# A two-layer hybrid decoder on one core: the 16 operand tiles of the activations, each 64 bytes further into its 512 bytes than the last

## The chip, the cores and the metric

One core of a Trainium2 chip runs the whole program. The metric is device time in microseconds, from one launch to its end. In the profile PE is TensorE, PEld its weight loads, DVE VectorE, ACT ScalarE, POOL GpSimd and SP SyncE, which issues the loads of the weights.

## What is computed

Two decoder layers on 512 tokens of 1024 channels, float32. Each layer adds half of a SwiGLU feed-forward net (FFN) of the normalized residual, then a mixer (a state-space scan, sliding-window attention and a spatial gating unit, side by side), then half of a second FFN; a last RMSNorm ends it. From the reference:

```python
def swiglu(x, w_gate, w_up, w_down):
    return (jax.nn.silu(x @ w_gate) * (x @ w_up)) @ w_down
...
    for l in range(DEPTH):
        x = x + 0.5 * swiglu(rmsnorm(x, ffn1_norm[l]), ffn1_w_gate[l], ffn1_w_up[l], ffn1_w_down[l])
        h = rmsnorm(x, mix_norm[l])
        proj = h @ w_in[l]
...
        x = x + jnp.concatenate([y_ssd, y_att, y_sgu], axis=-1) @ w_out[l]
        x = x + 0.5 * swiglu(rmsnorm(x, ffn2_norm[l]), ffn2_w_gate[l], ffn2_w_up[l], ffn2_w_down[l])
    return rmsnorm(x, final_norm)
```

The width of a FFN is 2816 = 22 x 128.

## The kernel before

The residual stays in SBUF as eight tiles xT (L66), 128 channels on the partitions by 512 tokens. Weights come as tiles of 128 output channels: `load` (L106) fetches 128 x 1024 float32 into one of five buffers raw, and `split` (L119) makes of it a pair whi (ScalarE, L128) and wlo (VectorE, L129), four buffers each, whose sum is the weight. Activations are split the same way: `split_x` (L135) takes two buffers from `xtile` (L132) and writes xhi (ScalarE, L137) and xlo (VectorE, L138). Both kinds are float32r. `product` (L142) then sums, for each chunk of 128 input channels, three matmuls into one PSUM bank: xhi with whi (L148), xlo with whi (L149), xhi with wlo (L151). In each, the weights are the stationary operand (128 x 128, 512 bytes on a partition, loaded by a weight load of its own) and the activations the moving one (512 columns, 2048 bytes on a partition).

A stage takes 16 tiles from `xtile`, a hi and a lo for each of eight chunks, always in the order hi 0, lo 0, hi 1, lo 1 and so on: `prepare` (L196) and `prepare_first` (L204) for the two FFNs and the mixer's input projection, `finish` (L524) for its output projection. `in_products` (L212) takes the weight tiles one after another through the eight chunks: 44 tiles in a FFN, 20 (and one of 16 columns, wdt, L657) in a mixer's input projection, eight in its output projection. The FFN's second product uses the same `product` with tiles h (L310), 4096 bytes with hi and lo side by side, as the moving operand: 22 chunks for each of eight output tiles. In the last FFN that is replaced by `down_final` (L702): h is the stationary operand there, in pieces of 128 tokens, and whi or wlo the moving one (L722 to L724); it also takes two tiles fw from the activations' buffers for the weights of the last norm, which VectorE reads at L734.

Layout in SBUF: pools lie one behind another in the order const, wp, xp, rp, and then ff (an FFN) or mp (a mixer). wp holds 13 tiles of 4096 bytes (raw, whi, wlo). xp holds the eight xT and the 16 activation tiles, 2048 bytes each. rp holds five tiles of 2048 bytes and two tiles rcol of 16 bytes, which take 32 each. The tiles of ff, h among them, are multiples of 2048 bytes. The order of the instructions and all waits between engines come from the framework, which follows tiles: a tile that reuses a buffer waits for the last reader of the one before.

Of the kernel before, what the change touches and what calls it, by code (L numbers as in the profile page):

```python
"""Two hybrid decoder layers (macaron SwiGLU, SSD | sliding-window attention | chunked SGU) on one core.

The residual lives in SBUF, channels on partitions. Every weight product takes both operands as an
exact pair hi + lo of float32r numbers and sums hi*hi + hi*lo + lo*hi in float32 in PSUM. The scale
of a token's RMSNorm is applied to the product's rows instead of to its operand.
"""
# [11 lines left out]
F32 = mybir.dt.float32  # L18
F32R = mybir.dt.float32r
# [3 lines left out]
PSUM = bass.MemoryType.PSUM  # L23
# [12 lines left out]

# columns of the table of per-channel vectors, 128 channels each
COLS = ("ffn1_norm", "mix_norm", "ffn2_norm", "ssd_norm", "attn_out_norm", "sgu_out_norm", "sgu_ln_w", "conv_b",
# [3 lines left out]
    [0, 16, 16, 16, 8, 4, 4, 4, 16, 64, 8]).tolist()  # L42
# the order in which the tiles of the input projection are taken
XBC_AT, GV_AT, U_AT, Z_AT = 4, 12, 14, 16
# [3 lines left out]
def trunk(ctx: ExitStack, tc: tile.TileContext, a: dict, out: bass.AP, phases=None):  # L48
# [42 lines left out]
    def attention_bias(pool, tags):  # L91
        """One row of biases by distance, skewed through DRAM into a Toeplitz band."""
        relx = rp.tile([33, 4], F32, name="relx", tag="rcol", bufs=2)
        nc.gpsimd.memset(relx, 1.0)
        nc.sync.dma_start(out=relx[0:32, :], in_=a["rel_bias"])
        ohx = pool.tile([33, 384], F32, name="ohx", tag=tags[0])
        nc.sync.dma_start(out=ohx, in_=a["onehot"])
        for h in range(4):
            b = bank()
            nc.tensor.matmul(b[:, 0:384], relx[:, h:h + 1].broadcast_to([33, P]), ohx, start=True, stop=True)  # L100
            ext = pool.tile([P, 384], F32, name="ext", tag=tags[1 + h % 2])
            nc.vector.tensor_copy(out=ext, in_=b[:, 0:384])
            nc.gpsimd.dma_start(out=skew[h].rearrange("(q i) -> q i", i=385)[:, 0:384], in_=ext)

# [1 line left out]
    def load(view):  # L106
        """Weights as they come, up to 1024 columns."""
        n = view.shape[-1]
        raw = wp.tile([P, 1024], F32, name="raw", tag="raw", bufs=RAW)[:, :n]
        nc.sync.dma_start(out=raw, in_=view)  # L110
        return raw
# [3 lines left out]
    def pinned(i):  # L115
        """At the start the engines take things in the order of the loads."""
        return order[0](i)

    def split(raw, n=P, mid=None):  # L119
        """Columns of weights as hi and lo, [P, chunks, n]; in halves if there is something to do between them."""  # L120
        m = raw.shape[1]
        hi = wp.tile([P, 1024], F32R, name="whi", tag="whi", bufs=4)[:, :m]
        lo = wp.tile([P, 1024], F32R, name="wlo", tag="wlo", bufs=4)[:, :m]
        for i in range(2 if mid else 1):
            if i:
                mid()
            c = slice(i * m // 2, (i + 1) * m // 2) if mid else slice(0, m)
            pinned(nc.scalar.copy(out=hi[:, c], in_=raw[:, c]))  # L128
            pinned(nc.vector.tensor_tensor(out=lo[:, c], in0=raw[:, c], in1=hi[:, c].bitcast(F32), op=ALU.subtract))  # L129
        return tuple(t.rearrange("p (k n) -> p k n", n=n) for t in (hi, lo))  # L130

    def xtile(nm):  # L132
        return xp.tile([P, T], F32R, name=nm, tag="xs", bufs=16)

# [7 lines left out]
    def product(ps, wt, x, ks, first, last):  # L142
        """ps += W[k].T X[k] for (i, k) in ks; wt = (hi, lo) with k's place i on axis 1, x = list of (hi, lo)."""
        whi, wlo = wt
        mm = None
        for i, k in ks:
            xh, xl = x[k]
            nc.tensor.matmul(ps, whi[:, i, :], xh, start=(k == first), stop=False)  # L148
            mm = nc.tensor.matmul(ps, whi[:, i, :], xl, start=False, stop=(wlo is None and k == last))  # L149
            if wlo is not None:  # L150
                mm = nc.tensor.matmul(ps, wlo[:, i, :], xh, start=False, stop=(k == last))  # L151
        latest[0] = mm.ins
# [3 lines left out]
    def behind():  # L156
        """What follows goes to TensorE behind the products so far."""
        return tc.issue_after(latest[0])

    class Stat:  # L160
        """Sum of squares of channel chunks as they come, then 1/sqrt(mean + eps) per token."""
        def __init__(self):
# [23 lines left out]
        def spread(self):  # L186
            """1/sqrt(...) of every token on all partitions, in PSUM."""
            r = self.r
            bc = bank()
            with behind():  # L190
                for c in range(NB):
                    nc.tensor.matmul(bc[:, c * P:(c + 1) * P], r[:, c:c + 1].broadcast_to([P, P]), ident,  # L192
                                     start=True, stop=True)
            return bc

    def prepare(wrow):  # L196
        """The current residual times the norm's weight as hi/lo operands, and its sum of squares."""
        st = Stat()
        xs = [split_x(xT[j], vcol(wrow + j)) for j in range(KD)]
        for j in range(KD):  # L200
            st.add(xT[j])
        return xs, st

    def prepare_first(wrow, js, xs, st):  # L204
        """The same for chunks js while the residual comes in."""
        for j in js:
            xs.append(split_x(xT[j], vcol(wrow + j)))
        if js[-1] == KD - 1:
            for j in range(KD):
                st.add(xT[j], nc.gpsimd if j < 4 else nc.vector)  # L210

    def in_products(tiles, xs, emit, hooks, levels=None, feed=None, ready=2, lead=3):  # L212
        """One product for each maker in tiles (-> (hi, lo), rows); the first lead ones go through the operand's
        chunks level by level, so that the last chunks may come late. hooks[v, n] is called before tile n's
        part of level v, feed before a level but the first; what emit needs is there before tile number ready ends."""
        levels = levels or [list(range(KD - 2)), [KD - 2, KD - 1]]
# [33 lines left out]

# [1 line left out]
    def ffn(l, which, first=False, fin=False):  # L252
# [82 lines left out]

# [1 line left out]
    def mixer(l):  # L337
# [3 lines left out]
        with tc.tile_pool(name="mp", bufs=1) as mp:  # L341
# [5 lines left out]

            # parameters of this layer
            bm = mp.tile([P, 4, 256], F32, name="bm")
# [24 lines left out]

# [1 line left out]
            dt, av, acs, cd, dtde = (small(n, 32) for n in ("dt", "av", "acs", "cd", "dtde"))  # L376
# [152 lines left out]

# [1 line left out]
            kT = t512("kT")  # L531
# [68 lines left out]

# [1 line left out]
            gn = mp.tile([P, NB, 256], F32, name="gn")  # L602
# [47 lines left out]

# [1 line left out]
            def mk_cols(i):  # L652
# [37 lines left out]

# [1 line left out]
            def mk_o(j):  # L692
# [9 lines left out]
    def down_final(dv, h):  # L702
        """out = rmsnorm(x + h W) with tokens on partitions, all of its sums in PSUM at once."""
        fw = [xp.tile([P, 512], F32, name=f"fw{i}", tag="xs", bufs=16) for i in range(2)]
        for i in range(2):
# [54 lines left out]
def one_hot_buckets():  # L760
    """Which bucket a distance has (the reference's static table), as one-hot columns between masked ends."""
    buckets, far = 32, 128
    n = np.arange(P)
    exact = buckets // 2
    large = exact + (np.log(np.maximum(n, 1) / exact) / np.log(far / exact) * (buckets - exact)).astype(np.int32)
    bucket = np.where(n < exact, n, np.minimum(large, buckets - 1))
    oh = np.zeros((33, 3 * P), np.float32)
    oh[32, :P] = NEG
    oh[32, 2 * P:] = NEG
    oh[bucket[::-1], P + n] = 1.0  # L770
    return oh


def laid_out(inputs):
    """The inputs as the kernel reads them: weights in tiles of 128 output channels, each with its chunks of
    128 input channels one after another on a partition; the residual with channels on partitions."""
    inp = {n: np.asarray(v) for n, v in inputs.items()}

    def tiles(w):
        """[..., K, N] -> [..., N / P, P, K / P * P]"""  # L780
        k, n = w.shape[-2:]
# [41 lines left out]
```

## Time and profile before

| | us |
|---|---|
| median of 2 runs | 1887.45 |
| range of the runs | 1886.72 to 1888.17 |
| span of the profiled execution | 1886.8 |

The profile is of one execution. Its page gives the busy time of every engine, the chain of work that ended last and the costliest groups of instructions; the trace behind it can be asked for the instructions in order of time (the timeline), for a table of stretches, and for one line of the code. Matmuls overlap at their ends, so the busy time of one is longer than the distance from its start to the start of the next.

### The profile page before, as it was taken

How to read it: one execution, taken by the hardware profiler on the slowest of the kernel's cores; microseconds unless marked ns; L12 is line 12 of the kernel's file. 1: busy time of each engine (PE TensorE's matmuls, PEld its weight loads, DVE VectorE, ACT ScalarE, POOL GpSimd, SP SyncE). 2: the span in 40 equal slices, each digit the busy share in tenths (PEclk: the TensorE clock that was granted, in tenths of full speed). 3: DMA queues.
4: the chain of work that ended last, by engine and by line, in shares of the span. 5: the costliest groups of instructions: out<-in, count | busy, mean ns of one | idle time of the engine just before them, and what ended most of it. 6: DMA issues, size and time to landing. Idle time of an engine off the chain costs nothing.

```text
span 1886.8 us, 21326 instructions
## 1 busy us (share of the span) xinstructions
PE 1868.9 (99%) x8608; PEld 1527.5 (81%) x8608; DVE 874.1 (46%) x1203; ACT 632.5 (34%) x854; POOL 127.9 (7%) x126
## 2 busy tenths in 40 slices
PE   8999999999999999999999999999999999999998
PEld 6888888877888888888888888887778888888886
DVE  6444433368855433433344344333787554444222
ACT  4323322247443322322223233223564432232112
POOL 2000000010221000000000000001102200000000
PEclk9999999999999999999999999999999999999999
DMA  5222333342222232233322323333422223223231
GB/s 210 100 100 90 98 92 93 97 141 70 79 87 99 91 101 99 89 92 99 102 91 99 101 91 93 92 90 110 123 89 69 90 90 101 96 94 101 79 100 45
DMA packets 54926, 182.78 MB, mean 97 GB/s; under 512 B 7211, under 2 KB 9196, under 8 KB 54828
## 3 DMA queue, kind: packets, MB, share of 16 engines
q1 hardware_dynamic: 49484, 172.37, 28.2%
q0 software_dynamic: 1920, 6.59, 1.2%
q10 hardware_dynamic: 3424, 2.46, 0.4%
q8 instruction: 68, 1.11, 0.2%
q14 instruction: 30, 0.25, 0.0%
HBM read 178.48 MB, written 2.92 MB: 96 GB/s over the span
## 4 chain that ended last, share of the span: by engine, by line
PE 94%; DVE 2%; DMA 1%; issue 1%; ACT 1%; POOL 0%; POOLq 0%; SPq 0%; ACTq 0%; DVEq 0%
PE accb L148 28%; PE accb L149 28%; PE accb L151 28%; PE mxb L723 1%; PE mxb L724 1%; PE mxb L722 1%; PE accb L723 1%; PE accb L722 1%; PE accb L724 1%; DMA acb<-arow 1%; PE mxb L179 1%; PE mxb L492 0%; PE mxb L192 0%; PE mxb L588 0%; PE mxb L641 0%
## 5 line engine op out<-in xcount | busy, mean ns | idle before, releaser
L148 PE MATMUL accb<-xhi,whi 128*128 128x512 f32 x1856 | 728.5, 393 | 5.9 <-ACT xhi L137 5.9
L149 PE MATMUL accb<-xlo,whi 128*128 128x512 f32 x1856 | 727.2, 392 | 0.5 <-DVE xlo L138 0.5
L151 PE MATMUL accb<-xhi,wlo 128*128 128x512 f32 x1856 | 726.5, 391 | 0.0
L128 ACT CAST whi<-raw 128x1024 fp32r<-128x1024 f32 (+1 forms) x322 | 333.1, 1037 | 1077.5 <-PE accb L149 619.3
L129 DVE TENSOR_TENSOR wlo<-raw,whi 128x1024 fp32r<-128x1024 f32 (+1 forms) x322 | 387.5, 1206 | 302.6 <-ACT whi L128 293.1
L148 PEld LDWEIGHTS accb<-xhi,whi 128*128 128x128 f32 x1856 | 350.0, 189 | 78.7 <-ACT xhi L137 6.1
L149 PEld LDWEIGHTS accb<-xlo,whi 128*128 128x128 f32 x1856 | 349.6, 188 | 75.1 <-DVE xlo L138 2.6
L151 PEld LDWEIGHTS accb<-xhi,wlo 128*128 128x128 f32 x1856 | 349.7, 188 | 73.1 <-issue 1.0
L148 PE MATMUL accb<-h,whi 128*128 128x512 f32 x528 | 208.0, 394 | 0.0
L151 PE MATMUL accb<-h,wlo 128*128 128x512 f32 x528 | 207.0, 392 | 0.0
L149 PE MATMUL accb<-h,whi 128*128 128x512 f32 x528 | 204.9, 388 | 0.0
L307 DVE TENSOR_TENSOR t<-accb,t 128x512 f32<-128x512 f32 x88 | 60.8, 691 | 273.3 <-PE accb L151 273.2
L302 DVE TENSOR_TENSOR t<-accb,R 128x512 f32<-128x512 f32 x88 | 60.5, 691 | 204.0 <-PE accb L151 203.9
L172 POOL TENSOR_TENSOR sqs<-sqs,sq 128x512 f32<-128x512 f32 x48 | 74.9, 1561 | 1118.9 <-ACT sq L171 1117.7
L151 PEld LDWEIGHTS accb<-h,wlo 128*128 128x128 f32 x528 | 99.1, 188 | 23.2
L149 PEld LDWEIGHTS accb<-h,whi 128*128 128x128 f32 x528 | 99.1, 188 | 22.2
L148 PEld LDWEIGHTS accb<-h,whi 128*128 128x128 f32 x528 | 99.3, 188 | 19.7
L313 DVE TENSOR_TENSOR h<-t,h 128x512 fp32r<-128x512 f32 x88 | 60.3, 685 | 3.4 <-ACT h L312 3.4
L312 ACT CAST h<-t 128x512 fp32r<-128x512 f32 x88 | 54.7, 621 | 19.1 <-DVE t L309 16.7
L303 ACT ACTIVATE t<-t 128x512 f32<-128x512 f32 x88 | 55.1, 627 | 3.8 <-DVE t L302 3.5
L333 DVE SCALAR_TENSOR_TENSOR t<-accb,R 128x512 f32<-128x512 f32 x24 | 16.6, 692 | 57.7 <-PE accb L151 57.7
L138 DVE SCALAR_TENSOR_TENSOR xlo<-xT,col,xhi 128x512 fp32r<-128x512 f32 x48 | 40.7, 866 | 2.4 <-ACT xhi L137 2.4
(203 smaller groups left out, 1088.9 us busy)
## 6 DMA issues: line engine op xcount, KB each, us to landing
raw<-in_ffn_w_gate_dram SPq DMA_DIRECT2D x86, 512.0 KB, 3.3
raw<-in_ffn_w_up_dram SPq DMA_DIRECT2D x86, 512.0 KB, 3.3
raw<-in_ffn_w_down_dram SPq DMA_DIRECT2D x48, 512.0 KB, 3.5
raw<-in_w_in_dram SPq DMA_DIRECT2D x40, 512.0 KB, 3.3
raw<-in_last_w_down_dram SPq DMA_DIRECT2D x22, 512.0 KB, 3.3
raw<-in_ffn_w_down_dram SPq DMA_DIRECT2D x24, 384.0 KB, 3.1
raw<-in_w_out_dram SPq DMA_DIRECT2D x16, 512.0 KB, 3.3
acb<-arow POOLq DMA_DIRECT2D x8, 512.0 KB, 6.1
```

The lines of the kernel that those rows point to most:

```text
L128: pinned(nc.scalar.copy(out=hi[:, c], in_=raw[:, c]))
L129: pinned(nc.vector.tensor_tensor(out=lo[:, c], in0=raw[:, c], in1=hi[:, c].bitcast(F32), op=ALU.subtract))
L138: pinned(nc.vector.scalar_tensor_tensor(out=lo, in0=src, scalar=w, in1=hi.bitcast(F32), op0=ALU.mult, op1=ALU.subtract))
L148: nc.tensor.matmul(ps, whi[:, i, :], xh, start=(k == first), stop=False)
L149: mm = nc.tensor.matmul(ps, whi[:, i, :], xl, start=False, stop=(wlo is None and k == last))
L151: mm = nc.tensor.matmul(ps, wlo[:, i, :], xh, start=False, stop=(k == last))
L172: eng.tensor_tensor(out=self.s, in0=self.s, in1=q, op=ALU.add)
L302: nc.vector.tensor_tensor(out=t, in0=b, in1=R, op=ALU.mult)
L303: nc.scalar.activation(out=t, in_=t, func=AF.Silu)
L307: nc.vector.tensor_tensor(out=t, in0=b, in1=t, op=ALU.mult)
L312: nc.scalar.copy(out=hi, in_=t)
L313: nc.vector.tensor_tensor(out=lo, in0=t, in1=hi.bitcast(F32), op=ALU.subtract)
```

## The change

The 16 buffers of one tag become 16 tags, xs0 to xs15, of one buffer each, and `xtile` hands them out in turn. Each buffer is 16 elements wider than the tile that is used of it: 2112 bytes, which is 4 x 512 + 64. So each of the 16 starts 64 bytes further into its 512 bytes than the one before; the places repeat after eight. The two tiles fw take their buffers from `xtile` too. Pools behind xp start 1024 bytes later. Comments and docstrings are removed; they leave empty lines, so lines ahead of `xtile` keep their numbers and those behind it are five later.

```diff
-    def xtile(nm):
-        return xp.tile([P, T], F32R, name=nm, tag="xs", bufs=16)
+    places = [0]
+
+    def xtile(nm, n=T, dtype=F32R):
+
+        i = places[0] % 16
+        places[0] += 1
+        return xp.tile([P, T + 16], dtype, name=nm, tag=f"xs{i}", bufs=1)[:, 0:n]
...
-        fw = [xp.tile([P, 512], F32, name=f"fw{i}", tag="xs", bufs=16) for i in range(2)]
+        fw = [xtile(f"fw{i}", 512, F32) for i in range(2)]
```

## Rows read from the trace of the kernel before

**Rows 1.** The page: the span, and engines with busy us (share of the span) xinstructions.
```profile
span 1886.8 us, 21326 instructions
...
PE 1868.9 (99%) x8608; PEld 1527.5 (81%) x8608; DVE 874.1 (46%) x1203; ACT 632.5 (34%) x854; POOL 127.9 (7%) x126
```

**Rows 2.** The page: the chain that ended last, by engine and by line.
```profile
PE 94%; DVE 2%; DMA 1%; issue 1%; ACT 1%; POOL 0%; POOLq 0%; SPq 0%; ACTq 0%; DVEq 0%
PE accb L148 28%; PE accb L149 28%; PE accb L151 28%; PE mxb L723 1%; PE mxb L724 1%; PE mxb L722 1%; PE accb L723 1%; PE accb L722 1%; PE accb L724 1%; DMA acb<-arow 1%; PE mxb L179 1%; PE mxb L492 0%; PE mxb L192 0%; PE mxb L588 0%; PE mxb L641 0%
```

**Rows 3.** TensorE's waits: who waited for whom: us in total, times, longest us.
```profile
PE accb L148 <- ACT xhi L137: 5.9, 1, 5.9
```

**Rows 4.** The page, costliest groups: count | busy us, mean ns | idle before, releaser.
```profile
L148 PE MATMUL accb<-xhi,whi 128*128 128x512 f32 x1856 | 728.5, 393 | 5.9 <-ACT xhi L137 5.9
```

**Rows 5.** Table of stretches: us, TensorE busy (instructions), granted clock, DMA share, GB/s.
```profile
60.00:240.00 180.00, 180.00 (x796) 1.00 0.29 96
...
600.00:800.00 200.00, 200.00 (x884) 1.00 0.30 99
840.00:920.00 80.00, 80.00 (x351) 1.00 0.32 97
...
1770.00:1870.00 100.00, 100.00 (x430) 1.00 0.22 69
```

**Rows 6.** Timeline of TensorE, activation products: start us, duration us, what.
```profile
700.21 0.39 PE L148 MATMUL accb<-xhi,whi 128*128 128x512 f32 x1
700.44 0.39 PE L149 MATMUL accb<-xlo,whi 128*128 128x512 f32 x1
...
702.25 0.39 PE L148 MATMUL accb<-xhi,whi 128*128 128x512 f32 x1
```

**Rows 7.** Timeline of TensorE, h products.
```profile
280.09 0.39 PE L149 MATMUL accb<-h,whi 128*128 128x512 f32 x1
280.32 0.39 PE L151 MATMUL accb<-h,wlo 128*128 128x512 f32 x1
280.55 0.39 PE L148 MATMUL accb<-h,whi 128*128 128x512 f32 x1
280.78 0.39 PE L149 MATMUL accb<-h,whi 128*128 128x512 f32 x1
```

**Rows 8.** Timeline of TensorE, last stage.
```profile
1760.22 0.40 PE L724 MATMUL mxb<-wlo,h 128*128 128x512 f32 x1
1760.46 0.39 PE L722 MATMUL mxb<-whi,h 128*128 128x512 f32 x1
1760.69 0.40 PE L723 MATMUL mxb<-whi,h 128*128 128x512 f32 x1
```

**Rows 9.** Table of stretches, then timeline of TensorE, behind a stall in the second mixer.
```profile
1347.50:1350.00 2.50, 2.50 (x7) 0.50 0.00 0
...
1347.56 0.63 PE L151 MATMUL accb<-xhi,wlo 128*128 128x512 f32 x1
...
1349.70 0.63 PE L149 MATMUL accb<-xlo,whi 128*128 128x512 f32 x1
```

**Rows 10.** Timeline of TensorE, a mixer's first products.
```profile
376.69 0.40 PE L148 MATMUL accb<-xhi,wdt 128*16 128x512 f32 x1
...
379.47 0.40 PE L148 MATMUL accb<-xhi,whi 128*128 128x512 f32 x1
...
380.62 0.39 PE L151 MATMUL accb<-xhi,wlo 128*128 128x512 f32 x1
```

**Rows 11.** Line L137: durations ns min/median/max; idle us before it and times, until what.
```profile
L137 ACT ACTIVATE xhi<-xT,col x48: 706/723/727, 5.1 to 1511.0; 128x512 fp32r<-128x512 f32 x48
...
  DVE xT L334: 15.6, 24
```

**Rows 12.** Lines L432 and L302: durations ns min/median/max.
```profile
L432 DVE TENSOR_TENSOR xc<-accb,R x16: 678/685/693, 413.4 to 1395.0; 128x512 f32<-128x512 f32 x16
...
L302 DVE TENSOR_TENSOR t<-accb,R x88: 680/692/693, 31.7 to 1744.6; 128x512 f32<-128x512 f32 x88
```

## The prediction, made before the changed kernel was run

> **What bounds the kernel now.** I read the page first. TensorE is busy for 1868.9 of 1886.8 us [rows 1], and the chain that ended last runs 94% over TensorE, 84% of it on three lines, L148, L149 and L151, the three products of one chunk [rows 2]. TensorE's waits say how little of that is waiting: the longest, 5.9 us, is the start of the kernel, and they stand in order of size [rows 3]. So the time is a count of matmuls times the distance from the start of one to the start of the next (its spacing), and any change that touches the spacing goes to the end undiluted. The groups by line give the count: L148 with an activation operand runs 1856 times, L149 and L151 as often, 5568 in all; 4 x 1056 = 4224 of them in the four FFN input stages (44 weight tiles x 8 chunks x 3), the other 1344 in the mixers [rows 4].
>
> The duration of a matmul in the groups (393 ns) is not its spacing, since neighbours overlap. The spacing comes from the table of stretches: an instruction counts there if any part of it lies inside, so a stretch of 180 us holds (180 + 0.39)/spacing of them. 796 in 60 to 240 us make 226.6 ns, 884 in 600 to 800 us 226.7; for the FFN output products (h as the moving operand) 351 in 840 to 920 us make 229.0 ns; for the last stage (weights as the moving operand, h as the stationary one) 430 in 1770 to 1870 us make 233.5 ns [rows 5]. The timeline shows the same, and how regular it is: activation products start every 0.226 to 0.227 us, nine spacings in 2.04 us [rows 6]; h products repeat 0.23, 0.23, 0.22 [rows 7]; the last stage alternates 0.23 and 0.24 [rows 8]. All have 512 columns, at a granted clock of 1.00 [rows 5]. [...]
>
> **Where they lie, from the code.** Tiles of wp and xp are whole multiples of 512 bytes, so every xs tile begins at the same place in its 512 bytes as every whi, wlo and raw tile, and so does each 512-byte chunk of weights: distance 0, spacing 226.7. Between xp and the tiles h lie the rp tiles, all multiples of 512 but the two small rcol, 32 bytes each: h sits 64 further. An h product therefore reads its moving operand 64 ahead of its weights (229.0), the last stage 64 behind (233.5). Within the activation stages the 16 buffers and the eight chunks are used in changing order and the spacing stays 226.7, so whole multiples of 512 do not matter, or not much.
>
> **The change part by part.**
>
> *The place.* With the stride of 2112 bytes tile i starts 64i further: hi of chunk k lies 128k and lo 128k + 64 ahead of the weights, modulo 512. The eight distances 0, 64, ... 448 occur evenly over hi and lo, and successive matmuls no longer have one distance. Three of the eight have a row: 0 (226.7), +64 (229.0), +448 which is -64 (233.5). For the other five no row exists. [...] Between them I take the middle of the two nearest off-zero places, 231.2. That is also what a product shows whose distance changes from chunk to chunk, though its stationary operand has 16 columns: wdt, whose chunks advance by 64 bytes, makes twelve spacings from 376.69 to 379.47 us, 231.7 ns, with the moving operands unmoved [rows 10]. Mean over eight: (226.7 + 229.0 + 233.5 + 5 x 231.2)/8 = 230.7, or +4.0 ns.
>
> How many feel it: the 4224 of the FFN stages in full. In the mixers other matmuls keep breaking in; after such a break the spacings are longer at first, 0.230 on the mean of the five from 379.47 to 380.62 us [rows 10], so I count half of 1344, 672. Together 4896 x 4.0 = +19.6 us. [...]
>
> [...]
>
> *The writers.* ScalarE (L137) and VectorE (L138) write the moved tiles, 64 times each, and they wait for their source (the residual, 15.6 us) and for no buffer [rows 11]. VectorE writes xc tiles, which are 2060 bytes wide and so start at other places, in 685 ns, the t tiles in 692 [rows 12]: the place costs a writer nothing. Bounds +/-10 ns x 64, under 1 us, and behind products already in flight in most stages.
>
> *The tags.* Sixteen tags of one buffer instead of one tag of sixteen: a tile now waits for the tile 16 before it rather than for any free one. Each stage takes 16 and frees them in the order it took them, so the buffer that is due is also the one that comes free first; L137 waits for no buffer now [rows 11]. Taken as 0. Without that cover it is one late split at each of four changeovers in the mixers, twice 0.72 us for hi and lo by L137, 6 us in all [rows 11]. fw takes places 0 and 1, whose tiles are long finished; its 2 loads and 8 readers are unchanged. All later pools move up by 1024 bytes, a multiple of 512: h and the last stage keep 229.0 and 233.5. No instruction or DMA is added or removed.
>
> Sum: 1886.8 + 19.6 = 1906.4, so 1906 us. The profiled execution, 1886.8, lies 0.65 us under the median of the runs, 1887.45, and inside their range, so I carry nothing over.
>
> **The rivals.**
>
> [...]
>
> [...]
>
> [...]
>
> *Much slower (1931 us).* No spacing settles and all run at 0.236: +45 us.
>
> **How the numbers follow.** Slower by 4 to 7 ns a matmul or a little less, 1893 to 1923 us: 0.52. Nothing, 1882 to 1892: 0.22. Faster: 0.18, of which 0.10 lies below 1850. Much slower: 0.08, nearly all above 1925. Two per cent, about what a measurement of this kernel can tell from no change, is 38 us: 1849.7 and 1925.2. So faster 0.10, slower 0.10, same 0.80. The range must leave out no more than 0.2: from 1864, which gives up most of the faster case, to 1927: 0.52 + 0.22 + about 0.06. The likeliest case's own range is 1893 to 1923.
>
> **What would show it.** [...] Spacing should then vary with the chunk number and repeat every four chunks, since 4 x 128 = 512. h products must stay at 351 in 80 us and the last stage at 430 in 100 us; if these move, my reading of the places is wrong. A wait of L137 for a buffer in the mixers would show the tags. The prediction fails if the five places without a row lie well off 231.

## The result

The changed kernel takes 1907.47 us (median of 2 runs, 1906.64 to 1908.31) against 1887.45 before: a ratio of 1.011, 95% interval 1.0093 to 1.0126. It is slower by 1.1%, 20.0 us, inside what a 2% bound calls the same, but clear of no change. The forecast was 1906 us.

The page of the changed kernel, span, engines, the chain by line, and the three costliest groups (count | busy us, mean ns | idle before). Lines behind `xtile` are five later: L148, L149 and L151 are L153, L154 and L156 now.

```profile
span 1906.6 us, 21310 instructions
...
PE 1890.3 (99%) x8608; PEld 1526.2 (80%) x8608; DVE 872.2 (46%) x1203; ACT 631.9 (33%) x854; POOL 126.3 (7%) x126
...
PE accb L156 28%; PE accb L153 28%; PE accb L154 28%; PE mxb L729 1%; PE mxb L728 1%; PE mxb L727 1%; PE accb L729 1%; PE accb L728 1%; PE accb L727 1%; DMA acb<-arow 1%; PE mxb L197 1%; DVE cv L442 1%; PE mxb L184 0%; PE mxb L497 0%; PE mxb L646 0%
...
L153 PE MATMUL accb<-xhi,whi 128*128 128x512 f32 x1856 | 731.8, 394 | 6.2 <-ACT xhi L142 6.2
L156 PE MATMUL accb<-xhi,wlo 128*128 128x512 f32 x1856 | 735.6, 396 | 0.0
L154 PE MATMUL accb<-xlo,whi 128*128 128x512 f32 x1856 | 732.5, 395 | 0.5 <-DVE xlo L143 0.5
```

Nothing has joined or left the kernel: 8608 matmuls and 99% of the span on TensorE, as in [rows 1], the same three lines in the chain, 28% each [rows 2], 1856 of each of them with an activation operand (L148 in [rows 4]). The kernel is still bound by the spacing of its matmuls, and the table of stretches shows it (us, TensorE busy and instructions, granted clock, DMA share, GB/s; the columns of [rows 5]). The first two lines are activation products of the first and second FFN, the third h products, the fourth the last stage:

```profile
60.00:240.00 180.00, 180.00 (x780) 1.00 0.28 95
...
620.00:800.00 180.00, 180.00 (x781) 1.00 0.27 96
840.00:940.00 100.00, 100.00 (x439) 1.00 0.32 99
...
1800.00:1860.00 60.00, 60.00 (x259) 1.00 0.29 97
```

780 or 781 instructions in 180 us make (180 + 0.39)/780 = 231.3 ns and 231.0 ns; before it was 796, 226.6 ns [rows 5]. The h products stay at 100.39/439 = 228.7 ns and the last stage at 60.39/259 = 233.2 (229.0 and 233.5 in [rows 5]). The granted clock is 1.00 in all these stretches. The starts themselves, which the trace gives to 1 ns, make a mean of 231.1 ns in the second FFN's input products against 226.7 before.

Where the time went, by the first start of each stage's products in the two timelines (a stage's products are counted off, 24 for each weight tile): the three later FFN input stages take 4.6 us longer each. The first ends 5.5 us later, of which 1.5 lies in its first 50 us, where this execution has a stretch at a granted clock of 0.50, behind eight matmuls of the attention bias (L100):

```profile
39.00:41.00 2.00, 2.00 (x6) 0.50 0.84 295
```

In the profile of before the same kind of stretch lies in the second mixer instead [rows 9]. Each of the two costs about 1.6 us, eight products that by the starts lie about 427 ns apart instead of 227 or 231, so they cancel in the total. The input projections of the two mixers differ by +1.3 and -1.0 us, the latter with that lower-clock stretch gone. In each of the two, activation products that follow one another without a break start 231.5 ns apart, where it was 228.3 before. From the first product of an output projection to the first of the next FFN it is 0.1 us more: its products take 0.7 us more, and the breaks between them 0.6 us less. The h stages and the last stage take the same time to 0.1 us. Sum: 5.5 + 3 x 4.6 + 1.3 - 1.0 + 2 x 0.1 = 19.8 us, the difference of the two spans, 1906.6 and 1886.8.

### The profile page after: what moved, and what is told of

The parts are those of the page before. It is cut to its first block, busy times and chain, and to the rows that moved or that the text cites. A ratio compares the mean times of both kernels' runs of the same rounds, so it can differ in the third digit from the quotient of the medians.

```text
span 1906.6 us, 21310 instructions
## 1 busy us (share of the span) xinstructions
PE 1890.3 (99%) x8608; PEld 1526.2 (80%) x8608; DVE 872.2 (46%) x1203; ACT 631.9 (33%) x854; POOL 126.3 (7%) x126
## 4 chain that ended last, share of the span: by engine, by line
PE 95%; DVE 2%; DMA 1%; issue 1%; ACT 0%; POOL 0%; POOLq 0%; SPq 0%; ACTq 0%; DVEq 0%
PE accb L156 28%; PE accb L153 28%; PE accb L154 28%; PE mxb L729 1%; PE mxb L728 1%; PE mxb L727 1%; PE accb L729 1%; PE accb L728 1%; PE accb L727 1%; DMA acb<-arow 1%; PE mxb L197 1%; DVE cv L442 1%; PE mxb L184 0%; PE mxb L497 0%; PE mxb L646 0%
## 5 line engine op out<-in xcount | busy, mean ns | idle before, releaser
L153 PE MATMUL accb<-xhi,whi 128*128 128x512 f32 x1856 | 731.8, 394 | 6.2 <-ACT xhi L142 6.2
L156 PE MATMUL accb<-xhi,wlo 128*128 128x512 f32 x1856 | 735.6, 396 | 0.0
L154 PE MATMUL accb<-xlo,whi 128*128 128x512 f32 x1856 | 732.5, 395 | 0.5 <-DVE xlo L143 0.5
L153 PEld LDWEIGHTS accb<-xhi,whi 128*128 128x128 f32 x1856 | 349.8, 188 | 86.4 <-ACT xhi L142 6.4
L154 PEld LDWEIGHTS accb<-xlo,whi 128*128 128x128 f32 x1856 | 349.0, 188 | 85.3 <-DVE xlo L143 2.6
L156 PEld LDWEIGHTS accb<-xhi,wlo 128*128 128x128 f32 x1856 | 349.0, 188 | 78.2 <-issue 1.0
L153 PE MATMUL accb<-h,whi 128*128 128x512 f32 x528 | 208.0, 394 | 0.0
L156 PE MATMUL accb<-h,wlo 128*128 128x512 f32 x528 | 207.0, 392 | 0.0
L154 PE MATMUL accb<-h,whi 128*128 128x512 f32 x528 | 204.9, 388 | 0.0
L156 PEld LDWEIGHTS accb<-h,wlo 128*128 128x128 f32 x528 | 99.1, 188 | 23.2
L154 PEld LDWEIGHTS accb<-h,whi 128*128 128x128 f32 x528 | 99.1, 188 | 22.2
L153 PEld LDWEIGHTS accb<-h,whi 128*128 128x128 f32 x528 | 99.3, 188 | 19.7
L317 ACT CAST h<-t 128x512 fp32r<-128x512 f32 x88 | 54.7, 622 | 19.6 <-DVE t L314 17.0
```

The lines of the kernel that those rows point to most:

```text
L317: nc.scalar.copy(out=hi, in_=t)
```

## The experiments

In every kernel below only places in SBUF and the order of buffers differ. In the stretches shown 180.39, 100.39, 80.39 or 60.39 us divided by the number of instructions is the spacing. "Distance" is that of the moving operand's place from the weights' place.

**The tags without the places.** Edit against the changed kernel:

```diff
-        return xp.tile([P, T + 16], dtype, name=nm, tag=f"xs{i}", bufs=1)[:, 0:n]
+        return xp.tile([P, T], dtype, name=nm, tag=f"xs{i}", bufs=1)[:, 0:n]
```

> Undoes the place alone: 16 tags of one buffer each as in the changed kernel, fw from the same places, but every tile 2048 bytes wide again, so all 16 lie at distance 0 from the weights. If the place is the whole cause (my step), 884 matmuls in 600 to 800 us, 226.7 ns, and 1887 us within 2 us. If the tags, the order of the buffers or the fw tiles carry a part of the 20 us, the time stays above 1890 us.

Measured: 1885.91 us, ratio to before 0.9992 (0.9983 to 1.0002). The first FFN's input products, in the table of stretches:

```profile
60.00:240.00 180.00, 180.00 (x796) 1.00 0.30 96
```

796 instructions, 226.6 ns. The tags and the order of the buffers carry none of the 20 us; the places carry it all. Against this kernel the places cost 21.6 us; that the tags alone save 1.5 us is not clear of noise.

**All 16 moved together by 64 bytes.** Edit against the kernel before:

```diff
-    xT = [xp.tile([P, T], F32, name=f"xT{j}") for j in range(KD)]
+    xT = [xp.tile([P, T + (16 if j == KD - 1 else 0)], F32, name=f"xT{j}")[:, 0:T] for j in range(KD)]
...
-            self.s = rp.tile([P, T], F32, name="sqs", tag="sqs", bufs=2)
+            self.s = rp.tile([P, T + 56], F32, name="sqs", tag="sqs", bufs=2)[:, 0:T]
```

> One tag of 16 buffers as before, but all 16 tiles moved together by 64 bytes; what lies behind them is moved by 512 in all, so h keeps its place. Distance theory (the spacing of a matmul is set by how far its moving operand lies from the weights, modulo 512): activation products take the spacing of the h products, 229.0 ns, 875 matmuls in 600 to 800 us, and the time rises by 2.3 ns x 4896 = 11 us to 1899 us. Succession theory (the spacing is set by how the place changes from one moving operand to the next, and one place for all is free): 226.7 ns, 884 matmuls, 1887 us.

Measured: 1897.72 us, ratio 1.0055 (1.0038 to 1.0072). Input products of the first FFN, then its h products:

```profile
60.00:240.00 180.00, 180.00 (x788) 1.00 0.29 94
270.00:370.00 100.00, 100.00 (x439) 1.00 0.31 94
```

228.9 and 228.7 ns: at the same distance the two kinds of product take the same spacing, down to the repeat of three, 232, 226 and 229 ns, that only h products had before. (It is in the starts to 1 ns; the steps of [rows 7] all round to 0.23 us.) The time is 1.3 us from the distance theory's 1899. One place for all is not free, so the succession theory as put there falls.

**Each distance by itself.** In two kernels each FFN gets its operand tiles in a pool of its own, at one distance per FFN; h follows at the same distance. The core of the edit against the changed kernel, where `g` is the gap, in elements, ahead of the first tile:

```diff
+        g = gap[0] if i == 0 else 0
-        return xp.tile([P, T + 16], dtype, name=nm, tag=f"xs{i}", bufs=1)[:, 0:n]
+        return xsp[0].tile([P, T + g], dtype, name=nm, tag=f"xs{i}", bufs=1)[:, g:g + n]
```

> Each FFN has its operand tiles in a pool of its own, all 16 of a stage at one distance from the weights, and the h tiles of the stage at the same distance: 64, 128, 192 and 256 bytes in the four FFNs in their order (the mixers at 64). [...] Succession theory: 226.7 ns in all four FFNs, whatever the distance. Read by stretches, not by the total.

> The same with the distances 320, 384, 448 and 0 in the four FFNs. Distance theory: 233.5 ns at 448 and 226.7 at 0, and with the four of the run before a mean over the eight of 231.1 ns, which is what the changed kernel shows in 600 to 800 us (872 matmuls: 229.8 by stretch). At 0 the h products run at 226.7 and the last stage, whose h then lies at the place of its moving operand, at 226.7 too instead of 233.5. Succession theory: 226.7 ns in all four, h unchanged at 229.0, the last stage at 233.5.

Measured: totals of 1910.54 and 1912.34 us, one run each, not used further. Distances 64, 128, 192 and 256; in pairs the input and the h products of the four FFNs, but for the last FFN, whose second line is the last stage:

```profile
60.00:240.00 180.00, 180.00 (x788) 1.00 0.30 95
270.00:370.00 100.00, 100.00 (x439) 1.00 0.31 94
620.00:800.00 180.00, 180.00 (x776) 1.00 0.29 94
840.00:940.00 100.00, 100.00 (x432) 1.00 0.32 99
990.00:1170.00 180.00, 180.00 (x773) 1.00 0.29 94
1210.00:1290.00 80.00, 80.00 (x345) 1.00 0.32 93
1570.00:1740.00 170.00, 170.00 (x752) 1.00 0.29 96
1800.00:1860.00 60.00, 60.00 (x266) 1.00 0.27 88
```

Distances 320, 384, 448 and 0, the input products of each FFN and the last stage:

```profile
60.00:240.00 180.00, 180.00 (x788) 1.00 0.29 94
...
620.00:800.00 180.00, 180.00 (x776) 1.00 0.29 95
...
990.00:1170.00 180.00, 180.00 (x774) 1.00 0.29 94
...
1570.00:1740.00 170.00, 170.00 (x752) 1.00 0.30 96
1800.00:1860.00 60.00, 60.00 (x266) 1.00 0.30 94
```

At 64 the spacing is 228.9 ns, at 128 232.5, at 192 233.4, at 256 226.6; and again 228.9, 232.5, 233.1 and 226.6 for 320, 384, 448 and 0 (192 and 448 differ by one instruction; the starts make 233.3 ns of both). The law repeats after 256 bytes, not after 512, and h products follow it as well (228.7, 232.4, 80.39/345 = 233.0). The last stage is the cleanest test: its moving operands, the weights, lie where they lay before in both kernels; with its stationary operand at a multiple of 256 it makes 60.39/266 = 227.0 ns instead of 233.2. So it is the relation of the two operands that counts, and not where the moving one lies.

**Finer steps.** The same kernel with the distances 32, 224, 16 and 240.

> The pool for each stage again, with the distances 32, 224, 16 and 240 bytes in the four FFNs, input products and h products alike. Steps of 64 gave 226.8 at 0 and 256, 229.0 at 64, 232.4 at 128 and 233.4 at 192, the same again 256 further. If the loss goes with the distance inside 256 bytes without steps, 32 lies between 0 and 64 at about 227.9, 16 at 227.3, and 224 and 240 between 192 and 0 at 230.1 and 228.4. If it goes by whole lines of 64 bytes, 32 and 16 show 226.8 or 229.0, and 224 and 240 233.4 or 226.8. Below 226.8 nowhere, unless the best place lies between two steps; then a better kernel follows.

Measured: 1922.19 us (one run). Input products of the four FFNs, then the last stage:

```profile
60.00:240.00 180.00, 180.00 (x773) 1.00 0.29 94
...
620.00:800.00 180.00, 180.00 (x773) 1.00 0.28 94
...
990.00:1170.00 180.00, 180.00 (x773) 1.00 0.29 96
...
1570.00:1740.00 170.00, 170.00 (x750) 1.00 0.29 96
1800.00:1860.00 60.00, 60.00 (x267) 1.00 0.28 88
```

233.4 ns at 32, at 224 and at 16, and 170.39/750 = 227.2 at 240. Neither of the two shapes that were put forward fits: 16 and 32 are as bad as 192, worse than 64. No distance was found with a spacing below that of 0 and 256 (the last stage's 60.39/267 = 226.2 is the 227.0 of the runs above but for one instruction, which is 0.9 ns in a stretch of 60 us).

**hi at 0, lo at 256.** The hi tiles get a pool of their own between wp and xp, and xT7 is 64 elements wider, so that lo lies at 256:

```diff
-        return xp.tile([P, T], F32R, name=nm, tag="xs", bufs=16)
+        return (xhp if nm == "xhi" else xp).tile([P, T], F32R, name=nm, tag="xs", bufs=8)
```

> The hi tiles stay at distance 0, all lo tiles go to 256 (two pools, the residual between them; h keeps its place). If the loss depends on the distance modulo 256 alone, nothing changes: 226.8 ns in the FFNs, 884 matmuls in 600 to 800 us, 1887 us. If a change of place from one moving operand to the next costs by itself, the spacing rises towards the 231.2 of the changed kernel.

Measured: 1885.19 us (one run).

```profile
60.00:240.00 180.00, 180.00 (x796) 1.00 0.30 96
```

226.6 ns. Steps of 256 between successive operands cost nothing.

**hi at 0, lo at 128, or at 64.** The same edit with other widths.

> The hi tiles stay at distance 0, all lo tiles go to 128. If each matmul pays for its own distance, every third one pays 232.4 and the mean is (2 x 226.8 + 232.4) / 3 = 228.7 ns, 877 matmuls in 600 to 800 us. If mixing costs by itself (the changed kernel shows 231.2 where the mean over its places is 230.4), the mean lies above that, towards 231.

> The hi tiles at distance 0, all lo tiles at 64, h in its old place. Own distance: (2 x 226.8 + 229.0) / 3 = 227.5 ns, 882 matmuls in 600 to 800 us, about 1890 us. A cost of the change of place by itself, as with lo at 128 (233.4 where its own distances gave 228.7): above 229.0, the worse of its two distances.

Measured: 1915.42 and 1913.62 us (one run each). Lo at 128, the four FFNs:

```profile
60.00:240.00 180.00, 180.00 (x773) 1.00 0.29 95
...
620.00:800.00 180.00, 180.00 (x773) 1.00 0.29 94
...
990.00:1170.00 180.00, 180.00 (x773) 1.00 0.29 94
...
1570.00:1740.00 170.00, 170.00 (x738) 1.00 0.29 96
```

Lo at 64, the first FFN, then the h products of the second and third:

```profile
60.00:240.00 180.00, 180.00 (x778) 1.00 0.28 93
...
840.00:940.00 100.00, 100.00 (x438) 1.00 0.33 99
...
1210.00:1290.00 80.00, 80.00 (x345) 1.00 0.31 90
```

With lo at 128 the mean is 233.4 ns, not 228.7: above both of the distances that occur, 226.6 and 232.5. With lo at 64 it is 180.39/778 = 231.9, not 227.5. So a matmul does not pay for its own distance alone. With lo at 128 the two products in three that lie at distance 0 are slow as well: by the starts in the first FFN, L148, L149 and L151 (here one line later) take 236, 234 and 230 ns. And what is the same layout modulo 512 bytes can settle in two ways: with lo at 128 the last FFN runs at 170.39/738 = 230.9 ns where the other three run at 233.4; with lo at 64 the h products of the third FFN, unmoved, run at 233.0 (345 in 80 us) and those of the second at 229.2.

**One place per chunk.** The stagger of the changed kernel with hi and lo of a chunk at one distance, 128 bytes further from chunk to chunk:

```diff
-        return xp.tile([P, T + 16], dtype, name=nm, tag=f"xs{i}", bufs=1)[:, 0:n]
+        return xp.tile([P, T + 32 * (i % 2)], dtype, name=nm, tag=f"xs{i}", bufs=1)[:, 0:n]
```

> The stagger of the changed kernel with one thing less: hi and lo of a chunk lie at the same distance, 128 bytes further from chunk to chunk. Modulo 256 the distances are 0 and 128 in turn, three matmuls each. If each matmul pays for its own distance, the mean is (226.8 + 232.4) / 2 = 229.6 ns, 873 to 874 matmuls in 600 to 800 us. If a change of place from one moving operand to the next costs by itself, the mean lies above that, and less so than with hi and lo apart, since only one step in three changes the place.

Measured: 1912.75 us (one run).

```profile
60.00:240.00 180.00, 180.00 (x777) 1.00 0.28 93
```

180.39/777 = 232.2 ns, against 229.6 by own distances. That one step in three changes the place instead of all did not make it less than the changed kernel's 231.2: the second half of that expectation missed.

**The weights moved instead.** The wlo tiles go to a pool of their own behind rp, 128 bytes from whi; the activations stay:

```diff
-        lo = wp.tile([P, 1024], F32R, name="wlo", tag="wlo", bufs=4)[:, :m]
+        lo = wlp.tile([P, 1024], F32R, name="wlo", tag="wlo", bufs=4)[:, :m]
```

> The moving operands all keep one place; instead the wlo tiles are moved 128 bytes from the whi tiles, in a pool of their own. If only the succession of the moving operands counts, input products stay at 226.8 ns, 884 matmuls in 600 to 800 us. If it is the relation between moving operand and weights, one in three of which now lies at 128 (modulo 256), the mean is 228.7 ns by own distances, or 231 to 233.4 as with lo at 128. The h tiles lie at 128 from whi and 0 from wlo here, so the h products change too.

Measured: 1914.81 us (one run). The first FFN's input products and h products, and the last stage:

```profile
60.00:240.00 180.00, 180.00 (x781) 1.00 0.29 94
270.00:370.00 100.00, 100.00 (x430) 1.00 0.30 93
...
1800.00:1860.00 60.00, 60.00 (x264) 1.00 0.32 103
```

180.39/781 = 231.0 ns, with moving operands that all lie where they lay before. The relation to the weights is enough to lose it all. In the h products and in the last stage two matmuls in three now lie at 128 and one at 0, which by own distances makes 230.5 ns for both. The h products take more, 100.39/430 = 233.5, but the last stage takes less, 60.39/264 = 228.7. So a mixture does not always cost more than the mean of its parts.

**The changed kernel 64 bytes further.** All distances of the changed kernel plus 64, by a wider xT7:

> The changed kernel with all 16 tiles 64 bytes further: the same steps from operand to operand, but hi at 64 and 192, lo at 128 and 0 modulo 256, instead of hi at 0 and 128, lo at 64 and 192. By own distances, hi counted twice: (2 x (229.0 + 233.4) / 2 + (232.4 + 226.8) / 2) / 3 = 230.7 ns here against (2 x (226.8 + 232.4) / 2 + (229.0 + 233.4) / 2) / 3 = 230.1 in the changed kernel, which measures 231.2. If the steps alone set the spacing, 231.2 here too.

Measured: 1906.03 us (one run). The first two FFNs:

```profile
60.00:240.00 180.00, 180.00 (x784) 1.00 0.29 93
...
620.00:800.00 180.00, 180.00 (x781) 1.00 0.29 94
```

230.1 ns in the first FFN, below the 230.7 by own distances; 231.0 in the second and 230.9 to 231.3 in the others, which is what the steps alone would give. The first differs from the others with no difference in the layout modulo 512 bytes, as with lo at 128.

**A version that beats both.** The opposite of the change: 192 more bytes ahead of the h tiles, so that h too lies a multiple of 256 from the weights. Edit against the kernel before:

```diff
-            self.s = rp.tile([P, T], F32, name="sqs", tag="sqs", bufs=2)
+            self.s = rp.tile([P, T + 24], F32, name="sqs", tag="sqs", bufs=2)[:, 0:T]
```

> A version meant to beat both: as before, but 192 bytes are added ahead of the h tiles, so h too lies a multiple of 256 from the weights. Nothing else differs. Distance theory: h products 226.8 instead of 228.9 ns, 1584 of them, -3.4 us; the last stage 226.9 instead of 233.5 ns, 528 matmuls, -3.5 us; 1880.5 us in all, 0.37% faster. If the place doesn't matter there, 1887.4 us.

Measured: 1880.38 us (5 runs), ratio to before 0.9962 (0.9948 to 0.9976). Input products and h products of the first FFN, and the last stage:

```profile
60.00:240.00 180.00, 180.00 (x796) 1.00 0.30 96
270.00:370.00 100.00, 100.00 (x443) 1.00 0.31 96
...
1800.00:1860.00 60.00, 60.00 (x266) 1.00 0.16 53
```

h products run at 100.39/443 = 226.6 ns, the last stage at 227.0: the FFN input products, the h products and the last stage now all run at the lowest spacing seen. The time expected was 1880.5 us.

## Why the prediction was right, and where its steps were not

*What bounds the kernel.* Right: the difference lies in the spacing, and in the stages that use the moved tiles; 4 x 4.6 = 18.4 us of it in the four FFN input stages.

*Places matter, tags and writers do not.* Right for all three. The tags alone give 1885.91 us. ScalarE now does wait for TensorE's last reader of a buffer, L142 (L137 before) twice, 0.5 us together, of which no stage shows a trace. It writes a tile in the same time, 722 ns in the median against 723 [rows 11]:

```profile
L142 ACT ACTIVATE xhi<-xT,col x48: 706/722/728, 5.4 to 1526.1; 128x512 fp32r<-128x512 f32 x48
...
  PE accb L156: 0.5, 2
```

The h products and the last stage kept their spacing, as said.

*Distance 0 is the good place.* Right, and shown from both sides: moving all 16 tiles by 64 costs 10 us, moving only the stationary operand of the last stage to distance 0 takes its spacing from 233.2 to 227.0.

*The period of the places.* Wrong. I took 512 bytes from the wording of the change and the layout; it is 256. So 256 is as good as 0 and 448 is 192. The sign that I named, a pattern that repeats every four chunks, failed accordingly: in the starts of the changed kernel's second FFN it repeats every two, with mean spacings of 231.7, 228.3, 228.3, 233.4, 231.6 and 233.4 ns.

*231.2 ns for the five places without a row.* The measured five are 232.5, 233.4, 226.6, 228.9 and 232.5, mean 230.8. The choice held in size because its misses nearly cancel, which is luck: 256 lies 4.6 ns below it, 320 lies 2.3 below and 192 lies 2.2 above.

*The mean over eight.* Right in size, wrong as a mechanism, and the step of the prediction that failed. It let each matmul pay for its own distance. Weighted as they occur, hi twice, the measured distances make (2 x (226.8 + 232.4)/2 + (229.0 + 233.4)/2)/3 = 230.1 ns; the changed kernel shows 231.1, and lo at 128 shows 233.4 where the same rule gives 228.7. The wdt row [rows 10] was the better guide than the mean: a distance that changes from product to product loses the low spacing of the one good place. It was used only as a support.

*How many feel it.* 4896 x 4.0 = 19.6 us against 19.8, of parts that were each off. The FFNs lost 18.4 us instead of 16.9. Of the mixers' 1344 matmuls half was taken, 2.7 us; all of them feel it, by about 1.3 us in each input projection, where the spacing was 228.3 ns before, and 0.7 us in each output projection, 4 us together. Some 2.6 us of this do not show in the difference of the two spans: the breaks in the output projections, waits in the second mixer and the start were that much shorter than in the profile of before, and no term held them. The breaks in the output projections are as short with the tags alone, where the time from the first product to the next FFN is 45.4 us instead of 46.0, so this gain comes with the tags and not with the places. The total's nearness owes something to chance.

*The rivals.* "Nothing" falls: with the tags alone the spacing is 226.6 ns, with the places as well 231.1, and one tag with all 16 tiles moved together makes 228.9. In the last stage the spacing depends on where the two operands of a matmul lie to each other: 233.2 and 227.0 ns with only its stationary operand moved. "Faster" falls: by the starts no arrangement was below 226.7. The chance given to it, and with it the lower end of the range at 1864, rested on an estimate of the author's that no run shows. "Much slower" falls too: its 0.236 us is the longer of the two alternating steps of the last stage before, 0.24 in [rows 8] and 235 to 236 ns by the starts. It occurs as a single step with lo at 128 as well, and no mean was above 233.5.

*What stays open.* Why 256 bytes, why 16 and 32 are worse than 64, why one layout settles at 233.4 in three FFNs and at 230.9 in the fourth, and why mixtures lie above the mean of their parts in most cases and below it in two. Which of a tag's buffers meet may differ from stage to stage: wdt takes a buffer of whi (L657 before) and none of wlo. That moves places by whole multiples of 4096 bytes, and no run tested whether it matters. What makes the spacing depend on the relation of moving operand and weights was not shown. No run left out the weight loads, so whether it is the load under way or the weights in use is not told apart.

## What to carry to other kernels

On a kernel that is bound by matmuls, measure the start-to-start spacing per stage, not the duration of a matmul, and compare stages of the same shape: 4.4 ns of 227 there were 1% of the whole. For float32r matmuls like these, 128 x 512 at a granted clock of 1.00, lay moving and stationary tiles at one place modulo 256 bytes: here 226.6 ns, against 231.1 in the changed kernel. Small tiles between pools were enough to lose it (two of 32 bytes here, 228.7 to 229.0 ns in the h products), and 192 bytes of padding put it right (226.6, and 0.38% of the whole). Spreading operands over all places was no safe middle here: no mixture of different places modulo 256 ran below 228.7 ns, and most ran slower than the mean of their parts (233.4 against 228.7 with lo at 128).

## What the runs showed of the hardware that was not expected

Matmuls of 128 x 512 float32r at a granted clock of 1.00 started every 226.6 to 227.0 ns when moving and stationary operands lay at one place modulo 256 bytes, and every 228.7 to 233.5 ns at the other distances that were tried but 240 (227.2). Distances that alternate gave 228.7 to 233.5: above the mean of their own in the changed kernel (231.1 against 230.1) and with lo at 128 (233.4 against 228.7), below it in the last stage with wlo moved (228.7 against 230.5). The spacing of one layout was not unique: 233.4 and 230.9 ns (lo at 128), 229.2 and 233.0 (h products with lo at 64), 230.1 and 231.0 (the changed kernel 64 further) occur within one execution.
